# A hybrid layer (RWKV-7, S5, GLA, cross-attention, convolutional feed-forward) on one core: packed parameters, another order of the fillers, and two direct feed-forward pairs

## The chip, the core and the metric

One of the eight cores of a Trainium2 chip. PE is TensorE (matmul), DVE VectorE, ACT ScalarE, POOL GpSimd; SP issues most DMAs. The metric is the device time of one execution in microseconds.

## What is computed

One layer over x (1024 tokens x 1024) and mem (256 x 1024), all in float32:

```python
h = rms_norm(x, norm_mix)
p_rw, p_s5, p_gla, p_gate = split(h @ w_in)
y_rw  = rwkv7_mix(p_rw, ...)    # S = S*w + (S@-kk)(kk*a)^T + v k^T, per head of 64, along the tokens
y_s5  = s5_mix(p_s5, ...)       # 32 groups of 16 channels, 64 complex diagonal states each; gelu, glu
y_gla = gla_mix(p_gla, ...)     # chunked gated linear attention
gates = sigmoid(p_gate)         # three gates of 1024 columns
x = x + (sum_i gates_i * (y_i @ w_branch_i)) @ w_out
x = x + cross_attention(rms_norm(x, norm_xattn), rms_norm(mem, norm_mem), ...)
u = conv3(rms_norm(x, norm_ffn) @ w_up) + conv_b          # depthwise along the tokens
x = x + (silu(u[:, :2816]) * u[:, 2816:]) @ w_down
return rms_norm(x, norm_final)
```

## The kernel before

**Products.** Each float32 operand is split into a rounded part and a remainder (`hi`, `lo`), and a product is three: hi*hi, hi*lo, lo*hi (`mm3`, L163 to L165). A weight unit (`wunit`, L156) is a DMA into `wraw`, a cast on ACT into `whi` (L147), and a subtraction on DVE into `wlo` (L148). `fm_block` fills ps_fm, 128 columns x 1024 tokens, with 96/2 = 48 products of 128x512 from two units. PSUM holds two tiles of 128x1024 (`psd`: ps_fm, ps_q, ps_dn) and four of 128x512 (`psm`: most others). Small products of float32 operands as they are (S5's, RWKV's) go through PE in two passes.

**Stages.** (1) The opening, to about 75 us: keys and values of mem, norm and transposition of x into hT. (2) S5, to about 330: u blocks; then for each half of the groups the transposed input maps (hs, ps_ht), the driven states (ps_in), a scan on DVE (L538 to L541), for each of two quads the gains ga (seven DVE operations through `cmul`, L330 to L337 and L559), the short kernels (ps_k, kp, a round through DRAM into M), and the outputs ps_y. (3) GLA. (4) RWKV: `rw1`, the triangular solve `rw_solve` on DVE, and `rw2`: 16 groups of four chunks with the products vl, w1, x1, z (z = vl*w1 + w1, needs the evacuated vl and w1) and qm (needs the evacuated z, `qz`), then four steps on the state (ps_p, L1013 to L1016; L1019 and L1020 scale the state for the next), then a norm. (5) Output projection and attention. (6) Feed-forward up, as 22 pairs of blocks: pair 0 direct, pairs 1 to 21 in Winograd form (`wino_product`, 84 products a pair instead of 96). (7) The down projection.

**What sets the order.** The tile scheduler writes each engine's instructions into one fixed order from the program's order and priorities; each engine works them off in that order and waits for semaphores. So work that does not depend on a stage is written as a *filler* inside it: 24 gate blocks of 48 products (`gate_block`), 11 of them in S5 (`filler`), 3 in `rw1`, 10 after it beside the solve; in `rw2`, `fill()` puts in the branch products once for each group. L156's loads, the gates' stores and S5's small transfers share SP's queue.

**Small loads.** `vectors` loads 15 parameter vectors as rows, transposes them on PE (ps_v) and copies them to columns; `conv_consts` does the same for the convolution, `s5_states` for S5's parameters (ps_s, ps_c, ps_d). mem is loaded, and transposed by 16 PE transposes (ps_t).

Of the kernel before, what the change touches and what calls it, by code (L numbers as in the profile page):

```python
# [9 lines left out]
F32 = mybir.dt.float32  # L10
# [11 lines left out]
NB = NFF // 2  # L22
EPS = 1e-6
# [17 lines left out]
class Trunk:  # L41
# [44 lines left out]
    def vectors(self, p):  # L86


        nc, cp, A = self.nc, self.cp, self.A
        rows = [("nmem", A["norm_mem"], 8), ("nmix", A["norm_mix"], 8), ("mu", A["rw_mu"], 14), ("w0", A["rw_w0"], 4),  # L90
                ("a0", A["rw_a0"], 4), ("kk", A["rw_k_k"], 4), ("ka", A["rw_k_a"], 4), ("rk", A["rw_r_k"], 4),
                ("lnw", A["rw_ln_w"], 4), ("lnb", A["rw_ln_b"], 4), ("bglu", A["s5_b_glu"], 4),
                ("nxa", A["norm_xattn"], 8), ("nffn", A["norm_ffn"], 8), ("gkb", A["gla_gk_b"], 2), ("gnorm", A["gla_norm"], 1)]
        nrow = sum(n for _, _, n in rows)
        self.vc = cp.tile([128, nrow], F32, name="vc")
# [3 lines left out]
        self.vo = {}  # L99
        vr = [p.tile([n, 128], F32, name=f"vr{n}") for n in (16, nrow - 16)]  # L100

        def load(part, t, r0):
            for name, ap, n in part:
                o = self.vo[name] = sum(x[2] for x in rows[:[x[0] for x in rows].index(name)])
                flat = ap if len(ap.shape) == 1 else ap.rearrange("a b -> (a b)") if len(ap.shape) == 2 \
                    else ap.rearrange("a b c -> (a b c)")
                nc.sync.dma_start(t[o - r0:o - r0 + n, :], flat.rearrange("(n p) -> n p", p=128))

        def columns(t, r, n):
            ps = self.psm.tile([128, 512], F32, tag="m", name="ps_v")  # L110
# [150 lines left out]
    def start(self, pool):  # L261

        self.hT = self.new_T(pool, "hT")
        with ExitStack() as c2:
# [17 lines left out]
            mem = [load(self.A["mem"][0, tt * 128:tt * 128 + 128, :]) for tt in range(2)]  # L282
            other_vectors = self.vectors(p)

            self.mT = {(k, l): p.tile([128, 256], F32R, name=f"mT{k}{l}") for k in range(8) for l in range(2)}
            self.to_fm(mem, "nmem", lambda k, l: self.mT[k, l][:])
            self.mrs = scales(mem)
            ones = p.tile([128, 128], F32, name="ones")
            self.nc.gpsimd.memset(ones[:], 1.0)
            self.mrb = p.tile([128, 256], F32, name="mrb")  # L290
            dg = p.tile([128, 256], F32, name="dg")
            for i in range(2):
                self.nc.vector.tensor_scalar(dg[:, i * 128:i * 128 + 128], self.ident[:], self.mrs[:, i:i + 1], None, op0=ALU.mult)
            ps = self.psm.tile([128, 512], F32, tag="m", name="ps_rb")
            self.nc.tensor.matmul(ps[:, :256], ones[:], dg[:], start=True, stop=True)
            self.nc.scalar.copy(self.mrb[:], ps[:, :256])
# [8 lines left out]
            self.kv_k(0)  # L305
            self.kv_k(1)
            load_x()
# [3 lines left out]
            norm_half(0)  # L311
            self.kv_v(0)
            norm_half(1)
            for j in range(1, 4):
                self.kv_v(j)
# [41 lines left out]
    def s5(self, filler):  # L357
# [4 lines left out]
        with ExitStack() as c1:  # L362
            po = self.pool(c1, "s5o")
            YT = [po.tile([128, T], F32, name=f"s5yt{b}") for b in range(4)]
            with ExitStack() as c2:
                p = self.pool(c2, "s5p")
                self.s5_states(p, YT, KD, UD)
                filler()
# [15 lines left out]
    def s5_states(self, p, YT, KD, UD):  # L384
# [3 lines left out]
        rows = p.tile([48, 128], F32, tag="kp", name="s5rows")  # L388
        ls = p.tile([48, 2], F32, name="s5ls")
        nc.sync.dma_start(rows[0:16, :], A["s5_a_re"][0].rearrange("(g r) n -> g (r n)", r=2))  # L390
        nc.sync.dma_start(rows[16:32, :], A["s5_a_im"][0].rearrange("(g r) n -> g (r n)", r=2))
        nc.sync.dma_start(ls[32:48, :], A["s5_log_step"][0].rearrange("(g r) -> g r", r=2))
        v.tensor_copy(rows[32:48, :].rearrange("p (r n) -> p r n", r=2), ls[32:48, :].unsqueeze(2).to_broadcast([16, 2, 64]))
        ps = self.psm.tile([128, 512], F32, tag="m", name="ps_s5")
        nc.tensor.transpose(ps[:, :48], rows[:, :], ident[:48, :48])
        par = p.tile([128, 48], F32, name="s5par")
        v.tensor_copy(par[:], ps[:, :48])
        ar, ai, lst = par[:, 0:16], par[:, 16:32], par[:, 32:48]
        B = [p.tile([128, 16, 16], F32, name=f"s5b{i}") for i in range(2)]
        C = [p.tile([128, 16, 16], F32, name=f"s5c{i}") for i in range(2)]  # L400
        for i, (bn, cn) in enumerate((("s5_b_re", "s5_c_re"), ("s5_b_im", "s5_c_im"))):
# [4 lines left out]
            for t in range(4):  # L406
                nc.tensor.transpose(ps[0:64, t * 128:t * 128 + 128], cr[:, t, :], ident[:])
# [1259 lines left out]
```

## Time and profile before

| | |
|---|---|
| time, median of 3 runs | 2225.42 us (2224.3 to 2226.51) |
| profiled execution | 2228.63 us, span 2226.9 |
| busy | PE 95%, PE's weight loads 78%, DVE 65%, ACT 43%, POOL 9% of the span |
| mean granted TensorE clock | 0.988 of full speed |
| DMA | 286.65 MB, mean 129 GB/s |

The profile is of one execution. Busy time of an engine is an average over stages; a wait is put down to the instruction that ended it last. The granted clock is the share of TensorE's full 2.4 GHz that the chip gave it; its other level is 1.2 GHz (0.5).

### The profile page before, as it was taken

To read this page: it belongs to the slowest core of one execution; us is meant where nothing else is said; L and a number is where in the kernel's file an instruction comes from. 1 tells how busy PE (TensorE), PEld (TensorE's weight loads), DVE (VectorE), ACT (ScalarE), POOL (GpSimd) and SP (SyncE) were. 2 spreads that over 40 slices of the span, in tenths; PEclk is the share of its full clock that TensorE was granted. 3 is DMA by queue.
4 is the path that set the end of the run, shared out by engine and by line. 5 is a ranking of instruction groups with operands and counts; after the bars stand their busy time and mean duration, and the time that the engine had idled before them with its cause. 6 is when DMAs were issued, how large, how long until landed. Compare 5 with 4: busy or idle time off the path is not lost.

```text
span 2226.9 us, 29866 instructions
## 1 busy us (share of the span) xinstructions
PE 2123.9 (95%) x10704; PEld 1738.8 (78%) x10704; DVE 1447.8 (65%) x2870; ACT 961.0 (43%) x1667; POOL 196.3 (9%) x292
## 2 busy tenths in 40 slices
PE   7999989999999999999999999999899999988997
PEld 7878779888888888888788787877677777766886
DVE  7783733554667761667686656657777777777756
ACT  6324243553554431333343544446444444453452
POOL 1000000001211221002200000000011111110000
PEclk9999999999999999999999999999999999999999
DMA  7423331112334465665564232332565566588332
GB/s 246 137 88 95 94 97 54 29 52 67 134 112 128 135 186 152 171 157 141 136 214 148 87 104 72 89 119 81 137 157 159 139 150 128 123 241 286 104 96 102
DMA packets 318878, 286.65 MB, mean 129 GB/s; under 512 B 92532, under 2 KB 253129, under 8 KB 318729
## 3 DMA queue, kind: packets, MB, share of 16 engines
q1 hardware_dynamic: 291385, 207.64, 32.7%
q0 software_dynamic: 27344, 77.08, 12.7%
q8 instruction: 85, 1.39, 0.3%
q14 instruction: 64, 0.52, 0.1%
HBM read 190.32 MB, written 94.34 MB: 128 GB/s over the span
## 4 chain that ended last, share of the span: by engine, by line
PE 78%; DVE 10%; ACT 4%; DMA 4%; issue 2%; SPq 1%; DVEq 0%; ACTq 0%
PE ps_fm L163 10%; PE ps_fm L165 10%; PE ps_fm L164 10%; PE ps_q L1287 5%; PE ps_q L1288 5%; PE ps_q L1289 5%; PE ps_dm L1461 4%; PE ps_dn L1461 4%; PE ps_tm L163 3%; PE ps_tm L165 3%; PE ps_tm L164 3%; DVE wlo L148 2%; PE ps_g L868 1%; ACT whi L147 1%; DMA araw<-d_act 1%
## 5 line engine op out<-in xcount | busy, mean ns | idle before, releaser
L148 DVE TENSOR_TENSOR wlo<-wraw,whi 128x512 fp32r<-128x512 f32 (+1 forms) x318 | 219.7, 692 | 278.4 <-ACT whi L147 276.1
L147 ACT CAST whi<-wraw 128x512 fp32r<-128x512 f32 (+1 forms) x318 | 196.5, 619 | 472.0 <-PE ps_fm L164 283.0
L163 PE MATMUL ps_fm<-hT,whi 128*128 128x512 f32 x800 | 319.1, 399 | 0.0
L164 PE MATMUL ps_fm<-hT,whi 128*128 128x512 f32 x800 | 317.5, 397 | 0.0
L165 PE MATMUL ps_fm<-hT,wlo 128*128 128x512 f32 x800 | 317.4, 397 | 0.0
L163 PEld LDWEIGHTS ps_fm<-hT,whi 128*128 128x128 f32 x800 | 151.8, 190 | 33.1 <-issue 1.2
L165 PEld LDWEIGHTS ps_fm<-hT,wlo 128*128 128x128 f32 x800 | 151.5, 189 | 33.1 <-issue 0.6
L164 PEld LDWEIGHTS ps_fm<-hT,whi 128*128 128x128 f32 x800 | 151.8, 190 | 32.6 <-issue 0.8
L1287 PE MATMUL ps_q<-a,whi 128*128 128x512 f32 x336 | 134.9, 402 | 13.1 <-ACT u L1362 5.6
L1289 PE MATMUL ps_q<-a,wlo 128*128 128x512 f32 x336 | 134.1, 399 | 1.1 <-DVE wlo L148 1.1
L1288 PE MATMUL ps_q<-a,whi 128*128 128x512 f32 x336 | 134.0, 399 | 0.0
L1300 DVE SCALAR_TENSOR_TENSOR c<-u,cvn,c 128x1023 f32<-128x1023 f32 x84 | 107.7, 1283 | 22.2 <-ACT c L1298 20.8
L1309 POOL DMA_DIRECT2D d_act<-c x77 | 65.9, 862 | 438.5 <-DVE c L1304 320.5
L165 PE MATMUL ps_tm<-whi,a 128*128 128x512 f32 x256 | 101.3, 396 | 0.0
L1461 PE MATMUL ps_dn<-whi,b 128*128 128x512 f32 x312 | 98.6, 393 | 2.8 <-ACT whi L147 2.8
L147 ACT CAST whi<-s 128x512 fp32r<-128x512 f32 x84 | 52.1, 620 | 105.3 <-PE ps_q L1288 80.9
L147 ACT CAST b<-araw 128x512 fp32r<-128x512 f32 x72 | 44.7, 620 | 101.3 <-PE ps_dn L1461 37.6
L1287 PEld LDWEIGHTS ps_q<-a,whi 128*128 128x128 f32 x336 | 64.4, 192 | 29.5 <-ACT u L1362 6.9
L1461 PE MATMUL ps_dm<-whi,b 128*128 128x512 f32 x264 | 84.0, 398 | 2.4 <-ACT whi L147 2.4
L148 DVE TENSOR_TENSOR wlo<-s,whi 128x512 fp32r<-128x512 f32 x84 | 57.6, 688 | 36.3 <-ACT whi L147 35.3
L163 PE MATMUL ps_fm<-a,whi 128*128 128x512 f32 x192 | 78.7, 410 | 2.3 <-ACT whi L147 2.2
L148 DVE TENSOR_TENSOR b<-araw,b 128x512 fp32r<-128x512 f32 x72 | 49.6, 690 | 47.1 <-ACT b L147 46.9
(551 smaller groups left out, 5058.9 us busy)
## 6 DMA issues: line engine op xcount, KB each, us to landing
wraw<-in_w_in SPq DMA_DIRECT2D x104, 256.0 KB
araw<-d_act SPq DMA_DIRECT2D x77, 256.0 KB
d_act<-c POOLq DMA_DIRECT2D x22, 768.0 KB, 7.6
d_gate<-gate SPq DMA_DIRECT2D x24, 512.0 KB
gsg<-d_gate SPq DMA_DIRECT2D x24, 512.0 KB
wraw<-in_ffn_w_up SPq DMA_DIRECT2D x46, 256.0 KB
d_act<-c POOLq DMA_DIRECT2D x11, 1024.0 KB, 6.1
d_act<-c POOLq DMA_DIRECT2D x44, 256.0 KB, 5.1
```

Of the source, the lines that this page charges most:

```text
L147: self.nc.scalar.copy(hi, src)
L148: self.nc.vector.tensor_tensor(lo, src, hi.bitcast(F32), op=ALU.subtract)
L163: nc.tensor.matmul(ps, lh, rh, start=first, stop=False)
L164: nc.tensor.matmul(ps, lh, rl, start=False, stop=False)
L165: nc.tensor.matmul(ps, ll, rh, start=False, stop=last)
L868: nc.tensor.matmul(ps[:, j * 128:j * 128 + 128], BD[i][:, ci, :], AR[:, :, ci * 64:ci * 64 + 64], start=True, stop=True)
L1287: nc.tensor.matmul(ps, hi[:, s], t[0][:], start=first and k == 0, stop=False, skip_group_check=True)
L1288: nc.tensor.matmul(ps, hi[:, s], t[1][:], start=False, stop=False, skip_group_check=True)
L1289: nc.tensor.matmul(ps, lo[:, s], t[0][:], start=False, stop=last and k == 3, skip_group_check=True)
L1300: v.scalar_tensor_tensor(c[:, d:], src[:, :T - d], cw(2 - d), c[:, d:], op0=ALU.mult, op1=ALU.add)
L1309: to = lambda n0, n1, h, **kw: nc.gpsimd.dma_start(st(n0, n1), src[h].to_broadcast([128, n1 - n0, 512]), **kw)
L1461: nc.tensor.matmul(o, a[x][:, s], w[y], start=first and k == 0, stop=last and k == 2, skip_group_check=True)
```

## The change

1. *Packed parameters.* The host lays the 15 vectors out as one array of columns (128x81), the convolution's constants as another (128x176), S5's as a third (`s5_par`, 128x1076, 551 KB, the first load of all), and passes mem transposed (`memT`, 1 MB) beside mem. The transposes of these leave PE. Keys are copied out of PSUM at once, into eight tiles, and scaled and stored later.
2. *S5.* The gains and short kernels of both quads now come before the scan; 13 gate blocks (before: 11) stand at set places.
3. *RWKV.* `rw2_prods` is cut in three, with a filler behind x1 and one behind the norm; the step of the group before goes between z and qm.
4. *Feed-forward.* Two direct pairs, whose convolution reads PSUM itself; 20 Winograd pairs.
5. *Down projection.* The first bank of accumulators is in `psm`, the second in `psd`.

```diff
+ND = 2
...
     def vectors(self):
+        nc.sync.dma_start(self.vc[:], A["cols"])
...
+            raw = [p.tile([128, 2, 256], F32, name=f"memT{u}") for u in range(4)]
...
+                self.nc.scalar.mul(self.mT[k, 0][:], t, g)
+                self.nc.vector.scalar_tensor_tensor(self.mT[k, 1][:], t, g, self.mT[k, 0][:].bitcast(F32), op0=ALU.mult, op1=ALU.subtract)
...
-            o = self.st.tile([128, 256], F32, tag="ko", name="ko", bufs=2)
-            nc.vector.tensor_tensor(o[:], ps[:, :256], self.mrb[:], op=ALU.mult)
-            nc.gpsimd.dma_start(self.d_k[c:c + 128, :], o[:])
+            o = self.kvp.tile([128, 256], F32, tag="ko", name="ko", bufs=8)
+            (nc.vector.tensor_copy if q else nc.scalar.copy)(o[:], ps[:, :256])
+            self.keys.append(o)
...
     def s5_states(self, p, pk, YT, KD, UD, fill):
...
+            fill(2)
...
+            def kernels(qd):
...
+                return GA, M
+            GA, M0 = kernels(0)
+            G0 = gains(GA)
+            GA, M1 = kernels(1)
+            fill(3)
             X = S[:, :, :, 1:129]
...
+            fill(1)
             for qd in range(2):
...
+                G, M = (gains(GA), M1) if qd else (G0, M0)
...
                 for g2 in range(2):
-                    todo.append((pr, hf * 2 + g2, self.rw2_prods(p, g2 * 4, t, R, c3)))
-                    if len(todo) > 1:
+                    z, qm = self.rw2_prods(p, g2 * 4, t, R, c3)
+                    fill()
+                    z()
+                    if todo:
                         step()
+                    todo.append((pr, hf * 2 + g2, qm()))
+                    norm()
+                    fill()
...
+        for b in range(ND):
+            cs = []
+            for i in range(2):
+                blk = i * NFF + b
+                ps = self.fm_block(A["ffn_w_up"][0][:, blk * 128:blk * 128 + 128], rhs, 8, by_half=b == 0)
+                c = self.xt(6 - 2 * b + i, "c")
+                conv(b, i, ps, c, self.cv, ((0, 512), (512, T)) if b == 0 else ((0, T),))
+                cs.append(c)
+            finish(b, cs)
...
-            for b in range(1, NFF):
+            for b in range(ND, NFF):
...
-            upto = -(-len(early) * g // 13) if g <= 13 else len(early) + -(-len(late) * (g - 13) // 3)
+            upto = -(-len(early) * g // 26) if g <= 26 else len(early) + -(-len(late) * (g - 26) // 6)
...
-                    self.gate_block(*gates[11 + pr])
+                    self.gate_block(*gates[13 + pr])
...
-            for g in gates[14:]:
+            for g in gates[16:]:
```

In all PE has 18 instructions fewer (9717 for 9735, with 12 products more in the feed-forward block), DVE 13, ACT 7, and SP 19 DMAs fewer. The lines of the new kernel are some 20 to 34 lower.

How the order moves, at three places. DVE in S5's first half, at the end of the scan (sc, s5s), before; cm and ga are the gains, kp the kernels' evacuation:

```order
L538 TENSOR_TENSOR sc_1646<-s5s,s5l 128x16x63
L539 TENSOR_TENSOR sc_1647<-s5s,s5l 128x16x63
L540 TENSOR_TENSOR sc_1646<-sc_1646,sc_1647 128x16x63
L148 TENSOR_TENSOR wlo<-wraw,whi 128x512
L541 TENSOR_TENSOR s5s<-s5s,sc_1646 128x16x63
L331 TENSOR_TENSOR cm_1660<-s5pw_1190,s5c_1102 128x576
L330 TENSOR_TENSOR cm_1659<-s5pw_1189,s5c_1101 128x576
L332 TENSOR_TENSOR ga_1657<-cm_1659,cm_1660 128x576
L335 TENSOR_TENSOR cm_1664<-s5pw_1189,s5c_1102 128x576
L336 TENSOR_TENSOR cm_1665<-s5pw_1190,s5c_1101 128x576
L337 TENSOR_TENSOR ga_1658<-cm_1664,cm_1665 128x576
L559 TENSOR_SCALAR ga_1658<-ga_1658 128x576
```

and in the new order, ahead of the scan:

```order
L479 COPY s5s<-ps_in 128x2x2x128 x2
L312 TENSOR_TENSOR ga_1638<-cm_1640,cm_1641 128x576
L315 TENSOR_TENSOR cm_1645<-s5pw_1125,s5pk 128x576
L316 TENSOR_TENSOR cm_1646<-s5pw_1126,s5pk 128x576
L317 TENSOR_TENSOR ga_1639<-cm_1645,cm_1646 128x576
L486 TENSOR_SCALAR ga_1639<-ga_1639 128x576
L310 TENSOR_TENSOR cm_1681<-s5pw_1125,s5pk 128x576
L115 TENSOR_TENSOR wlo<-wraw,whi 128x512
L495 SCALAR_TENSOR_TENSOR kp<-e_1065,s5pk,ps_k 128x16
L496 COPY kp<-ps_k 128x112
L311 TENSOR_TENSOR cm_1682<-s5pw_1126,s5pk 128x576
L312 TENSOR_TENSOR ga_1679<-cm_1681,cm_1682 128x576
```

The gains and kp stood behind the scan; they now stand ahead of it, among the copies of the driven states.

PE in RWKV's second half, from one group's z to its first steps, before:

```order
L979 MATMUL ps_z<-qw_8188,qvl 128x128 x4
L163 MATMUL ps_fm<-a_7869,whi 128x512
L164 MATMUL ps_fm<-a_7870,whi 128x512
L165 MATMUL ps_fm<-a_7869,wlo 128x512
L163 MATMUL ps_fm<-a_7875,whi 128x512
L979 MATMUL ps_qm<-qz,wa_7939 128x128
L1013 MATMUL ps_p<-qx_8043,qz 128x128
L1014 MATMUL ps_p<-wv_7926,R_7969 128x128
L1016 MATMUL ps_p<-s_0_0_7952,qqm 128x128
L979 MATMUL ps_qm<-qz,wa_7939 128x128 x3
```

and in the new order, in a group of the first half (ps_fm is filler):

```order
L130 MATMUL ps_fm<-a_7848,whi 128x512
L131 MATMUL ps_fm<-a_7849,whi 128x512
L132 MATMUL ps_fm<-a_7848,wlo 128x512
L952 MATMUL ps_z<-qw_8615,qvl 128x128
L994 MATMUL ps_p<-qx_8490,qz 128x128
L995 MATMUL ps_p<-wv_7863,R_8451 128x128
L952 MATMUL ps_z<-qw_8615,qvl 128x128 x3
L994 MATMUL ps_p<-qx_8490,qz 128x128
L995 MATMUL ps_p<-wv_7863,R_8451 128x128
L997 MATMUL ps_p<-s_2_1_7899,qqm 128x128
```

The filler between z and qm is now ahead of z; between z and qm stand products of the step.

DVE in the feed-forward block, where pair 0's convolution (L1300, cv) and the u of the first Winograd pair (L1368) stand, before:

```order
L1300 SCALAR_TENSOR_TENSOR c_14352<-u_14063,cv,c_14352 128x1022
L148 TENSOR_TENSOR wlo<-s_14402,whi 128x512
L1300 SCALAR_TENSOR_TENSOR c_14356<-u_14127,cv,c_14356 128x1023
L1274 TENSOR_TENSOR s_14518<-b_0_1_14512,wraw 128x512
L1300 SCALAR_TENSOR_TENSOR c_14356<-u_14127,cv,c_14356 128x1022
L148 TENSOR_TENSOR wlo<-s_14406,whi 128x512
L1274 TENSOR_TENSOR s_14520<-s_14518,b_0_1_14510 128x512
L1274 TENSOR_TENSOR s_14522<-b_0_1_14510,b_0_1_14512 128x512
L1304 TENSOR_TENSOR c_14352<-c_14352,c_14356 128x1024
L1368 TENSOR_TENSOR u_14253<-ps_q,u_14399 128x512
L148 TENSOR_TENSOR wlo<-b_0_1_14510,whi 128x512
```

and in the new order, around the convolution of the last direct block (L1283, from PSUM):

```order
L1283 SCALAR_TENSOR_TENSOR c<-ps_fm,cv,c 128x1023
L115 TENSOR_TENSOR wlo<-s_14312,whi 128x512
L1283 SCALAR_TENSOR_TENSOR c<-ps_fm,cv,c 128x1022
L1255 TENSOR_TENSOR s_14459<-b_0_1_14361,wraw 128x512
L115 TENSOR_TENSOR wlo<-s_14314,whi 128x512
L1287 TENSOR_TENSOR c<-c 128x1024
L115 TENSOR_TENSOR a_14301<-t_14283,a_14300 128x512
L1334 TENSOR_TENSOR u_14322<-ps_14321,p_14340 128x512
```

The direct pairs' convolutions now precede the first Winograd sums' remainders; the u of the first Winograd pair (L1352) comes 11 rows behind these.

## Rows read from the trace of the kernel before

**Rows 1.** The page's first part: busy time of PE in us, its share of the span, and its instructions.

```profile
PE 2123.9 (95%) x10704; PEld 1738.8 (78%) x10704; DVE 1447.8 (65%) x2870; ACT 961.0 (43%) x1667; POOL 196.3 (9%) x292
```

**Rows 2.** PE's timeline: start and duration in us, engine, line, operation, out<-in. The first and the last start of 31 products of 128x512 that follow one another.

```profile
953.22 0.39 PE L165 MATMUL ps_fm<-a,wlo 128*128 128x512 f32 x1
...
960.16 0.39 PE L165 MATMUL ps_fm<-a,wlo 128*128 128x512 f32 x1
```

**Rows 3.** Busy time by stretches of the span (start:end, length; for each engine its busy us and its instructions; the mean granted clock of TensorE, DMA's busy share, GB/s).

```profile
0.00:75.00 75.00, 60.22 (x472) 58.02 (x473) 52.56 (x129) 48.75 (x89) 9.58 (x25) 1.00 0.74 229
75.00:330.00 255.00, 234.29 (x1208) 189.66 (x1207) 153.71 (x363) 84.41 (x119) 5.81 (x11) 0.96 0.33 96
880.00:1112.00 232.00, 219.65 (x1392) 186.31 (x1391) 159.38 (x395) 76.18 (x156) 27.10 (x28) 1.00 0.59 151
1537.00:1600.00 63.00, 51.98 (x201) 39.70 (x200) 50.76 (x76) 32.63 (x52) 3.99 (x5) 0.92 0.33 88
1950.00:2050.00 100.00, 88.57 (x358) 68.55 (x358) 71.75 (x102) 43.75 (x70) 10.05 (x12) 0.97 0.89 272
```

**Rows 4.** PE's waits by what ended them: us in total, how often, the longest.

```profile
PE ps_k L563 <- DVE ga L332: 9.9, 2, 5.1
...
PE ps_v L111 <- DMA vr<-in_norm_mix: 6.6, 1, 6.6
PE ps_qm L979 <- DVE qz L997: 6.1, 6, 2.3
...
PE ps_q L1287 <- DVE u L1368: 5.1, 1, 5.1
PE ps_t L254 <- DVE hn L1165: 4.6, 4, 3.9
...
PE ps_ht L513 <- DVE hs L332: 2.6, 1, 2.6
PE ps_fm L163 <- DVE ko L1114: 2.6, 3, 1.8
PE ps_y L586 <- DMA s5m<-s_k: 2.5, 1, 2.5
PE ps_q L1287 <- ACT whi L147: 2.5, 1, 2.5
...
PE ps_y L585 <- ACT s5g L577: 1.9, 1, 1.9
PE ps_fm L163 <- ACT s5h L147: 1.8, 1, 1.8
...
PE ps_z L979 <- DVE qw L990: 1.1, 3, 0.4
```

**Rows 5.** The same table as in rows 3, for two stretches of the opening and for the one in which DVE works out S5's parameters.

```profile
0.00:10.00 10.00, 1.73 (x7) 1.32 (x7) 3.63 (x19) 5.44 (x8) 1.73 (x11) 1.00 0.85 258
10.00:20.00 10.00, 9.18 (x60) 8.69 (x60) 6.91 (x22) 6.84 (x15) 0.00 (x0) 1.00 0.92 289
84.00:107.00 23.00, 23.00 (x100) 18.56 (x100) 20.38 (x119) 6.56 (x13) 1.09 (x2) 1.00 0.28 92
```

**Rows 6.** The timelines of DVE and of ACT around S5's scan in the first half: the scan's first operation, the first of ga after it (L331), and ACT's four copies of the scanned states.

```profile
129.52 1.23 DVE L538 TENSOR_TENSOR sc<-s5s,s5l 128x1024 f32<-128x1024 f32 x1
...
161.93 0.75 DVE L331 TENSOR_TENSOR cm<-s5pw,s5c 128x576 f32<-128x576 f32 x1
```

```profile
162.05 4.21 ACT L553 COPY s5s<-s5s 64x1024 f32<-64x1024 f32 x4 [5.91 <-DVE s5s L541]
```

**Rows 7.** The timeline of all engines in RWKV's second half: one link of the state (L1016 is the product with the state, L1019 and L1020 scale it), and a z with its qz and qm.

```profile
950.12 0.39 PE L1016 MATMUL ps_p<-s,qqm 128*128 128x128 f32 x2
...
950.61 0.29 DVE L1019 TENSOR_SCALAR s<-ps_p,rw_pc 64x64 f32<-64x64 f32 x1 [0.45 <-PE ps_p L1016]
...
950.93 0.31 ACT L1020 ACTIVATE s<-ps_p,rw_pc 64x64 f32<-64x64 f32 x1 [1.42 <-DVE s L1019]
...
951.84 0.39 PE L1016 MATMUL ps_p<-s,qqm 128*128 128x128 f32 x2
```

```profile
963.21 1.13 PE L979 MATMUL ps_z<-qw,qvl 128*128 128x128 f32 x8
...
964.38 0.69 DVE L997 TENSOR_TENSOR qz<-ps_z,qw 128x512 f32<-128x512 f32 x1 [1.31 <-PE ps_z L979]
...
965.13 0.49 PE L979 MATMUL ps_qm<-qz,wa 128*128 128x128 f32 x2
```

**Rows 8.** The timelines of POOL, of SP's queue and of PE ahead of RWKV's second half: the store of the solved triangles, the last load of the first group's ring, the first group's first product.

```profile
839.07 0.54 POOL L907 DMA_DIRECT2D rw_x<-sx  x1 [26.90 <-DVE sx L905]
```

```profile
860.22 0.63 SPq L962 DMA_DIRECT2D wv<-rw_tm  x1
```

```profile
884.33 1.05 PE L979 MATMUL ps_vl<-wx,wn 128*128 128x128 f32 x8
```

**Rows 9.** DVE's groups by line and shape (busy us, mean ns of one, idle time before) for RWKV's second half and for the feed-forward block; then the first Winograd product on PE, and DVE's operation that ended the longest wait in the block.

```profile
L1088 DVE TENSOR_TENSOR a<-gsg,ps_fm 128x512 f32<-128x512 f32 x16 | 10.3, 684 | 1.3 <-PE ps_fm L165 1.1
```

```profile
L148 DVE TENSOR_TENSOR wlo<-s,whi 128x512 fp32r<-128x512 f32 x84 | 57.6, 688 | 36.3 <-ACT whi L147 35.3 <-PE ps_q L1288 1.0
```

```profile
1546.43 0.42 PE L1287 MATMUL ps_q<-b,whi 128*128 128x512 f32 x1
```

```profile
1580.68 0.68 DVE L1368 TENSOR_TENSOR u<-ps_q,u 128x512 f32<-128x512 f32 x1
```

More of the change, by code (lines that the diff above doesn't have):

```diff
@@ L311, in start @@
             norm_half(0)
+            self.mrs = scales([load(self.A["mem"][0, tt * 128:tt * 128 + 128, :]) for tt in range(2)])
             self.kv_v(0)
             norm_half(1)
+            ones = p.tile([128, 128], F32, name="ones")
+            self.nc.gpsimd.memset(ones[:], 1.0)
+            mrb = p.tile([128, 256], F32, name="mrb")
+            dg = p.tile([128, 256], F32, name="dg")
+            for i in range(2):
+                self.nc.vector.tensor_scalar(dg[:, i * 128:i * 128 + 128], self.ident[:], self.mrs[:, i:i + 1], None, op0=ALU.mult)
+            ps = self.psm.tile([128, 512], F32, tag="m", name="ps_rb")
+            self.nc.tensor.matmul(ps[:, :256], ones[:], dg[:], start=True, stop=True)
+            self.nc.scalar.copy(mrb[:], ps[:, :256])
+            for j, o in enumerate(self.keys):
+                self.nc.vector.tensor_tensor(o[:], o[:], mrb[:], op=ALU.mult)
+                self.nc.gpsimd.dma_start(self.d_k[j * 128:j * 128 + 128, :], o[:])
             for j in range(1, 4):
@@ L355, in exp_exact, with s5 @@
         return q
-    def s5(self, filler):
+    def s5(self, c1, pk, fill):
         nc, A, v = self.nc, self.A, self.nc.vector
@@ L417, in s5_states @@
+        ar, ai, lst, dcol = (pk[:, o:o + n] for o, n in ((0, 16), (16, 16), (32, 16), (48, 4)))
+        B, C = ([pk[:, o + i * 256:o + i * 256 + 256].rearrange("p (g c) -> p g c", g=16) for i in range(2)] for o in (52, 564))
         e16 = p.tile([128, 16], F32, name="e16")
@@ L1496, in ffn_down @@
                 add(i, 0, bank["A"][i], ALU.add)
-            bank["B"] = [self.psm.tile([128, 512], F32, tag="m", name="ps_dm")[:] for _ in range(4)]
+            bank["B"] = second()
             product("s1", "n1", bank["B"], True, False, (load_w("b22"),))
@@ L1509, in ffn_down @@
                 add(4 + i, 1, bank["A"][i], ALU.subtract, True)
-            bank["B"] = [self.psm.tile([128, 512], F32, tag="m", name="ps_dm")[:] for _ in range(4)]
+            bank["B"] = second()
             product("a12", "b21", bank["B"], True, True)
@@ L1544, in run, with fill @@
         self.d_v = self.dr.tile([256, D], F32, name="d_v")
-        self.start(self.pool(left, "hT"))
-        self.s5(lambda: [self.gate_block(*g) for g in gates[:11]])
+        hT, c1 = self.pool(left, "hT"), ExitStack()
+        pk = self.pool(c1, "s5k").tile([128, 1076], F32, name="s5pk")
+        nc.sync.dma_start(pk[:], A["s5_par"])
+        self.start(hT)
+        todo = gates[:13]
+        def fill(n):
+            for _ in range(min(n, len(todo))):
+                self.gate_block(*todo.pop(0))
+        self.s5(c1, pk, fill)
         self.gla()
```

256 lines of the change are left out of this document (103 added, 153 removed).

## The prediction

> **What bounds the kernel now.** I read the profile from the engines down to single waits. The page's first part gives the bound: PE is busy for 2123.9 us, 95% of the span of 2226.9 [rows 1]. The profiled execution took 2228.63 us, its span and 1.7 us around it, 3.2 us over the median of 2225.42; a term worked out from its trace is subtracted from the median. Where every cover holds, PE starts a 128x512 product each (960.16 - 953.22) / 30 = 0.231 us [rows 2]; so only three things shorten this kernel: fewer products, less waiting on PE, and less time at the half clock. The table by stretches says where the last two lie [rows 3]. From 75 to 330 us, the S5 stage, PE idles 255 - 234.3 = 20.7 us at a mean granted clock of 0.96; 4% of 255 us is another 10.2 us. In RWKV's second half (880 to 1112) it idles 12.4 us, in the opening 75 us 14.8, in the first part of the feed-forward block (1537 to 1600) 11.0 us, and there the clock of 0.92 costs 5.0 more. Around 1950 to 2050 DMA is 0.89 busy. [...]
>
> **The change part by part.**
>
> *Opening, +3 us.* Removed: 16 transposes of mem and the one of the gains (some 17 x 0.13 = 2 us of PE), and the waits on them: PE's first instruction came at 6.6 us behind a row load, and 2.6 us were lost on ko, whose evacuation waited for the scale [rows 4]. Now ko is a plain copy into eight buffers. Added: memT is loaded as well as mem (1.05 MB more), and the S5 block of 551 KB, formerly loaded later in pieces, stands first on SP's queue. That is 1.6 MB where DMA ran at 258 to 289 GB/s [rows 5]: 6 us if nothing hides it. In the new SP order 4 x loads (2.1 MB) also stand ahead of the third key block's weights; 0.55 + 1.05 + 1.05 + 2.1 + 0.26 MB at 0.27 MB/us is 18 us, some 5 us after PE would be done with two blocks. The queue's later half has room (0.74 busy over 75 us, rows 3). PE's idle of 14.8 us should become about 14, and the work 2 to 3 us less; bounds -4 (all of the 6 us lost) and +7. The Trainium skill (DMA: Bandwidth & Descriptors, Specifications) limits one core to some 358 GB/s of HBM; no stretch here reaches that, and by it the 1.6 MB take an estimated 4.5 us, which would make this term +4.5.
>
> *S5, +20 us.* Before, DVE ran the scan from 129.52 to 161.93 us and only then the seven operations of ga, each 0.67 to 0.8 us start to start, for which ps_k waited 5.1 us; ACT's four copies of 4.21 us stood behind the scan, too [rows 6]. The 9.9 us at ps_k, 2.6 at ps_ht, 4.4 at ps_y and 1.8 at s5h make 18.7 of the 20.7 us [rows 4]. ps_ht now has 192 products (44 us) ahead of it; DVE's chain of parameters, which filled 20.4 us of it between 84 and 107 us [rows 5], takes some 30 us with the subtractions. At ps_k the new DVE order puts copies, two subtractions and three operations ahead of the first ga (some 5.6 us) against 11 products, 16 ps_in and 8 transposes (some 5.2 us): up to 0.5 us left, four times. ps_y stands 143 + 11 products behind the last kernel (35 us); scan with its subtractions and the copies are 32.4 + 4.2 = 36.6 us: 1 to 2 us left in each half, perhaps with one half clock (1.7 us). 40 products (9 us) now cover the s5h chain. Kept: 2 + 4 + 3 and 2 of small ones; 30.9 - 11 = 20. Bounds: 28 with nothing kept, 8 if each half keeps a 4 us stop and its clock at both ps_k and ps_y.
>
> *RWKV, +6 us, and -1 ahead of it.* qm starts 1.9 us after z's first product at the best (963.21 and 965.13, rows 7), since qz stands between them on DVE from 964.38 for 0.69 us; z itself takes 0.9 us of the 1.9. ps_qm's 6.1 us idle and its 2.3 us stop near 1108 with a half clock of 1.7 us are to be had, and 1.1 us of ps_z [rows 4]. But the new order puts the filler between x and z; behind z stand mostly one step of three products (0.67 us) and 0 to 3 fillers, so in half of the 16 groups some 0.4 us stays. 6.1 + 1.7 + 1.1 - 8 x 0.4 = 5.7. Bounds 0 and 11. Ahead of it two gate blocks fewer (96 products, 22 us) cover the triangular solve: before, its result left at 839.07, the last load of the first group's ring was issued at 860.22, PE arrived at 884.33 [rows 8]. It now arrives 22 us earlier, at 862: about 0 to 2 us of stop; taken 1, bounds 0 and 6.
>
> *Feed-forward, +11 us.* A second direct pair costs 96 products for 84, +12 x 0.231 = 2.8 us, less the about 1 us that each Winograd pair loses: +1.7. Gained: PE reached the first ps_q at 1546.43 and then stood 2.5 us for whi and 5.1 us for the u of L1368 [rows 4], which DVE ran at 1580.68, behind the convolution, sums and the 1024-wide product of pair 0 [rows 9]; these and small stops are the 11.0 us of the stretch [rows 3]. Gone are 10.4 of them and 4 of the 5.0 us of clock. With 96 products more ahead of it, PE gets there 22 us later, while DVE has 30 operations more at 0.6 and 1.2 us less 8 that move away: about 5 us in hand. The stop at hn (4.6 us in four, rows 4) keeps its order and stays. New: the convolution of the last direct block reads ps_fm until about 1577, and the second ps_q wants that bank at about 1577: 0 to 3 us, taken 1.5. 10.4 + 4 - 1.7 - 1.5 = 11; bounds 4 and 13. On that read: DVE's 128x512 operations take 684 ns with a PSUM source (L1088) and 688 ns without one (L148) [rows 9], so I charge nothing. The Trainium skill (VectorE: DVE Perf Modes, Rules for kernel authors) speaks against it: copy to SBUF first if there are many operations; by its table of fixed costs the 12 operations would take an estimated 0.065 us more each, and the sum would be 0.8 us less. The rows do not agree with that, and I follow them.
>
> *Down projection, 0.* The accumulators change places between two pools, but PE waited there for whi behind araw loads and order and loads are the same. Bounds -3 and +4. The constants' transposes near 1400 are two.
>
> Sum: 3 + 20 + 6 - 1 + 11 + 0 = 39 us; 2225.4 - 39 = **2186 us**.
>
> **The rivals.**
>
> *A, part of the stops form anew (-5 to -30, say 2206).* DVE takes its instructions in order; each cover above is within 1 to 2 us of what it covers, and a late first ga, a late scan and the bank at the second ps_q each bring the half clock back. For it: 32.6 us of filler against 36.6 us of scan. Against it: any single one costs 2 to 4 us. Three or four of them, and an opening bound by DMA, take 19 us: 2206.
>
> *B, slower.* The 60 links of RWKV's state go from ps_p over DVE's and ACT's s back to the next ps_p. At 950.12 and 951.84 a link takes 1.72 us on PE; its chain ends at 950.93 + 0.31 = 951.24 and, with a handover, needs some 1.25 us [rows 7]. The order now has seven links with only five small products between (1.34 us). If the spread fills put one 128x512 operation (0.69 us) ahead of s on either queue in every link, that is up to 60 x 0.69 = 41 us, and with a half clock here and there 45: it decides above 0.65 us a link, and the time is 2186 + 45 = 2231. Against it: s keeps its high priority, and most links keep 1.56 us and more.
>
> *C, nothing comes of it.* The filler is one stock: what S5 gets, the solve and the rest lose. It would take stops of 39 us elsewhere; the stretches that lend it (1112 to 1525, 540 to 880) hardly idle. Time 2225.
>
> *D, more than forecast.* All upper bounds but the opening's: 3 + 28 + 11 + 13 + 2 = 57 us, 2168.
>
> **How the numbers follow.** The forecast, -30 to -52 us, 0.58; A 0.23; D 0.08; C 0.05; B 0.06. The range takes the forecast and most of A: 2168 (D's figure) to 2212 (A with one more term lost). 0.2%, 4.5 us, is about what this measurement can tell from no change. Faster by more: 0.58 + 0.08 + 0.22 of A = 0.88; slower: B, 0.06; within it 0.06. The likeliest case decides the time, 2186.
>
> **What would show it.** In the trace of the changed kernel: ps_k's wait below 2 us in all and the S5 stretch's clock at 0.98 or more; ps_y's wait below 5 us; qm's idle halved while z's is gone; the first ps_vl without a stop over 2 us; no stop for the u of the first Winograd pair; the first product near 8 us and the last of the opening near 71. The prediction is wrong if ps_y or ps_k keeps a half clock in both halves, if ps_p waits for s in many links, or if the opening ends later than 75 us.

## The result and the profile after

The changed kernel takes **2209.87 us** (median of 4, 2208.78 to 2213.87) against 2225.97 (4 runs): a ratio of 0.9932, 95% interval 0.9918 to 0.9945. It is faster by 16 us where 39 were forecast. 2209.87 lies inside the range, near its upper end and near rival A's figure. The profiled execution took 2213.87 us, 4.0 over its median, so sizes of 4 us below are not read from this trace alone.

Boundaries on PE (the start of the last product of a kind) cut both profiled executions into the same stretches; all in us. One gate block is 11.05 (88.6 - 66.5 is two of them).

| stretch | before | after | gain |
|---|---|---|---|
| start to the last product with s5h | 330.0 | 327.1, with 2 more gate blocks | 2.9 + 22.1 |
| of it, the opening (last key and value product) | 74.0 | 73.2 | 0.7 |
| GLA and RWKV's first loop | 465.7 | 465.8 | -0.1 |
| gate blocks up to the first ps_vl | 88.6 | 66.5, 2 fewer | 0 |
| RWKV's second half and attention, to the last ps_pt | 558.9 | 571.5 | **-12.6** |
| to the last transpose of hn | 92.8 | 92.2 | 0.6 |
| feed-forward, to the last ps_q | 459.6 | 457.9 | 1.7 |
| down projection, to PE's last product | 220.7 | 220.0 | 0.7 |

So S5 gave 24.3 and RWKV's second half took half of it back. Of its 12.6 us some 5 belong to this one execution: two other executions with the same instructions in the same order there (e3 and e4 below) took 566.3 and 566.9. PE's line of the page's first part, against [rows 1]:

```profile
PE 2121.5 (96%) x10686; PEld 1741.7 (79%) x10686; DVE 1445.0 (65%) x2857; ACT 950.8 (43%) x1660; POOL 196.0 (9%) x292
```

The same stretches as in [rows 3], but for the feed-forward's, which begins 12 us earlier, as the block does now, and ends at the same time:

```profile
0.00:75.00 75.00, 60.62 (x458) 58.03 (x459) 53.03 (x132) 49.45 (x94) 9.33 (x25) 0.98 0.78 243
75.00:330.00 255.00, 250.51 (x1310) 202.63 (x1309) 157.12 (x362) 86.13 (x123) 5.94 (x12) 1.00 0.36 105
880.00:1112.00 232.00, 215.82 (x1315) 186.41 (x1314) 160.17 (x390) 72.97 (x150) 27.02 (x28) 0.97 0.61 153
1525.00:1600.00 75.00, 66.54 (x268) 51.86 (x267) 56.40 (x83) 34.17 (x53) 5.28 (x6) 0.95 0.45 116
1950.00:2050.00 100.00, 89.98 (x360) 70.54 (x359) 75.89 (x114) 41.25 (x68) 8.03 (x10) 0.93 0.91 284
```

S5 idles 4.5 us for 20.7 and runs at the full clock. RWKV's second half idles 16.2 for 12.4 and its clock fell to 0.97. PE's waits, against [rows 4]:

```profile
PE ps_fm L130 <- ACT whi L114: 13.4, 4, 8.8
...
PE ps_p L994 <- ACT s L1001: 5.5, 8, 1.4
PE ps_z L952 <- DVE rs_b L193: 4.6, 2, 3.0
PE ps_t L221 <- DVE hn L1146: 4.5, 4, 3.9
...
PE ps_q L1268 <- DVE u L1352: 2.9, 1, 2.9
...
PE ps_y L551 <- ACT s5s L541: 2.5, 2, 1.2
...
PE ps_fm L130 <- DVE c L1283: 2.3, 1, 2.3
PE ps_z L952 <- DVE rs_y L194: 2.2, 2, 2.0
PE ps_z L952 <- DVE rs_b L192: 2.0, 1, 2.0
PE ps_qm L952 <- DVE qz L974: 1.8, 1, 1.8
PE ps_y L551 <- ACT s5g L507: 1.8, 2, 0.9
```

Of the first line, 8.8 us stand before the first product of all and 2.47 in the opening. ps_k, ps_ht, ps_v and ko are gone from the list, ps_qm fell from 6.1 to 1.8. New are ps_p behind s, ps_z behind the norm's rs_ operations, and two stops in the feed-forward block.

**How z comes to wait.** The timeline of after shows the longest of these (start, duration, engine, line, operation; in brackets the idle time before and what ended it):

```profile
1094.54 1.22 DVE L1081 TENSOR_TENSOR gsg<-gsg,ps_fm 128x1024 f32<-128x1024 f32 x1
1095.80 1.29 DVE L1083 TENSOR_TENSOR gsg<-gsg,a 128x512 f32<-128x512 f32 x2
1096.52 1.22 ACT L114 CAST a<-gsg 128x512 fp32r<-128x512 f32 x2 [3.03 <-DVE gsg L1083]
1097.17 0.69 DVE L115 TENSOR_TENSOR a<-gsg,a 128x512 fp32r<-128x512 f32 x1
1097.65 0.58 ACT L959 COPY qvl<-ps_vl 128x512 f32<-128x512 f32 x1
...
1099.31 0.68 DVE L963 COPY qw<-ps_w 128x512 f32<-128x512 f32 x1
...
1100.13 0.76 PE L952 MATMUL ps_z<-qw,qvl 128*128 128x128 f32 x2 [3.00 <-DVE rs_b L193]
...
1101.83 0.77 PE L130 MATMUL ps_fm<-a,whi 128*128 128x512 f32 x1
```

The filler behind the last norm has left its evacuations (gsg, the cast and the subtraction of a) on both queues, ahead of qvl and qw, which z needs. ps_w's products began at 1095.18, its copy qw only at 1099.31: eight small rs_ operations of the norm and four wide ones stand between. The slot between x and z, which should hide this, is empty here: 17 pieces of filler were dealt over 26 slots. Behind the stop a 128x512 product takes 0.77 us instead of 0.39; the granted clock is 0.50 until about 1106.

z's three other long stops (1.60 us at 981.30, 1.95 at 996.78, 1.96 at 1034.18) have a second cause. The timeline of after shows it at the middle one:

```profile
993.33 2.49 POOL L1073 TENSOR_TENSOR a<-a,gsg 128x512 f32<-128x512 f32 x2 [4.84 <-DVE gsg L1072]
993.75 0.87 DVE L190 TENSOR_SCALAR rs_y<-rs_i 64x8 int32<-64x8 int32 x1
994.66 1.18 DVE L192 TENSOR_TENSOR rs_b<-rs_y 64x8 f32<-64x8 f32 x1
995.87 0.16 DVE L193 SCALAR_TENSOR_TENSOR rs_b<-rs_x,rs_b 64x8 f32<-64x8 f32 x1
995.96 0.68 DVE L963 COPY qw<-ps_w 128x512 f32<-128x512 f32 x1
...
996.78 0.60 PE L952 MATMUL ps_z<-qw,qvl 128*128 128x128 f32 x2 [1.95 <-DVE rs_y L194]
```

POOL works on the filler's a in two operations of some 1.25 us. Two small operations of the norm, ahead of qw in DVE's queue, start beside them and take 0.87 and 1.18 us, where 0.16 is usual (the last section). By these rows that is an estimated 0.87 + 1.18 - 2 x 0.16 = 1.7 of the 1.95 us. No run took this work off POOL, so what it is worth in the whole is not shown.

**How u comes to wait.** POOL's, DVE's and PE's timelines of after, in the feed-forward block:

```profile
1569.27 1.37 POOL L1292 DMA_DIRECT2D d_act<-c  x2 [20.18 <-DVE c L1287]
1576.09 1.29 POOL L1292 DMA_DIRECT2D d_act<-c  x1 [5.45 <-DMA d_act<-c]
```

```profile
1584.69 0.69 DVE L1334 TENSOR_TENSOR u<-ps,p 128x512 f32<-128x512 f32 x1 [5.88 <-DMA d_act<-c]
...
1586.64 0.51 PE L1268 MATMUL ps_q<-a,whi 128*128 128x512 f32 x1 [2.91 <-DVE u L1352]
```

Direct pair 1 leaves its result in tiles 4 and 5, and the second Winograd pair's u is to be written to 4. That tile is free only when pair 1's store has left it: two transfers, then an accumulating one that waits for both and is issued 6.8 us later. DVE idles 5.88 us for it, the u of the first Winograd pair stands behind, and PE stops 2.91 us with a half clock after it. The other stop, near 1535, is a bank of PSUM: DVE's convolution of a direct block still reads ps_fm, and PE waits 2.3 us for it.

### The profile page after: what moved, and what is told of

Same layout as the page of the kernel before. It is cut to its first block, busy times and chain, and to the rows that moved or that the text cites. A ratio compares the mean times of both kernels' runs of the same rounds, so it can differ in the third digit from the quotient of the medians.

```text
span 2211.9 us, 29747 instructions
## 1 busy us (share of the span) xinstructions
PE 2121.5 (96%) x10686; PEld 1741.7 (79%) x10686; DVE 1445.0 (65%) x2857; ACT 950.8 (43%) x1660; POOL 196.0 (9%) x292
## 4 chain that ended last, share of the span: by engine, by line
PE 48%; DVE 5%; DMA 3%; ACT 2%; issue 1%; SPq 0%; DVEq 0%; ACTq 0%; POOLq 0%
PE ps_q L1268 5%; PE ps_q L1269 5%; PE ps_q L1270 4%; PE ps_dm L1439 4%; PE ps_dn L1439 4%; PE ps_fm L130 3%; PE ps_fm L131 3%; PE ps_fm L132 3%; PE ps_tm L130 2%; PE ps_tm L132 2%; PE ps_tm L131 2%; DMA araw<-d_act 1%; PE ps L1268 1%; ACT whi L114 1%; DMA wraw<-in_w_branch 1%
## 5 line engine op out<-in xcount | busy, mean ns | idle before, releaser
L115 DVE TENSOR_TENSOR wlo<-wraw,whi 128x512 fp32r<-128x512 f32 x320 | 220.6, 692 | 269.8 <-ACT whi L114 265.0
L114 ACT CAST whi<-wraw 128x512 fp32r<-128x512 f32 x320 | 197.2, 620 | 458.0 <-PE ps_fm L131 282.1
L1268 PE MATMUL ps_q<-a,whi 128*128 128x512 f32 x320 | 128.0, 400 | 7.6 <-ACT u L1346 4.2
L1269 PE MATMUL ps_q<-a,whi 128*128 128x512 f32 x320 | 127.2, 397 | 0.0
L1270 PE MATMUL ps_q<-a,wlo 128*128 128x512 f32 x320 | 126.7, 397 | 0.0
L1283 DVE SCALAR_TENSOR_TENSOR c<-u,cvn,c 128x1023 f32<-128x1023 f32 x80 | 102.5, 1283 | 19.4 <-ACT c L1280 18.2
L130 PE MATMUL ps_fm<-b,whi 128*128 128x512 f32 x192 | 77.9, 406 | 2.4 <-DVE c L1283 2.3
```

The lines of the kernel that those rows point to most:

```text
L114: self.nc.scalar.copy(hi, src)
L115: self.nc.vector.tensor_tensor(lo, src, hi.bitcast(F32), op=ALU.subtract)
L130: nc.tensor.matmul(ps, lh, rh, start=first, stop=False)
L1268: nc.tensor.matmul(ps, hi[:, s], t[0][:], start=first and k == 0, stop=False, skip_group_check=True)
L1269: nc.tensor.matmul(ps, hi[:, s], t[1][:], start=False, stop=False, skip_group_check=True)
L1270: nc.tensor.matmul(ps, lo[:, s], t[0][:], start=False, stop=last and k == 3, skip_group_check=True)
```

## The experiments

Three questions: what takes RWKV's second half down, what the feed-forward change is worth, and what the opening's stop costs. The stage below is the stretch from the first ps_vl to the last ps_pt. Shares "13/3/8" are gate blocks in S5, in RWKV's first loop, and behind it. In brackets behind a time stand its ratio to the kernel before, timed on the same chip, and the ratio's 95% interval; not all rounds ran on one chip, so runs are compared by these ratios.

**e1: the old dependent products in the changed kernel.**

```diff
-                    z, qm = self.rw2_prods(p, g2 * 4, t, R, c3)
-                    fill()
-                    z()
...
-            upto = -(-len(early) * g // 26) if g <= 26 else ...
+            upto = -(-len(early) * g // 13) if g <= 13 else ...
```

> The changed kernel with RWKV's second half as before (products undivided, one filler a group). Theory Q (queues): the split itself costs the 12.6 us that the stage is longer in the changed kernel, since the filler behind the norm sets branch evacuations and norm operations ahead of qw and qvl on DVE and ACT; time 2197 us (-12 to -14), ps_z's loss back at about 5 us. Rival P (place): the stage is longer because it starts 25 us earlier and finds its loads and the solve late; the split is worth its forecast +6, and undoing it gives 2209 to 2216.

Measured 2211.92 (2206.85 to 2214.23; 0.9946, 0.9931 to 0.9961), stage 566.0. Undoing the split gives nothing back. But it was no clean undoing: the same source as before's was laid out in another order on DVE and ACT, and there qm waits 9.9 us and z 7.5. PE's waits of e1 in the stage:

```profile
PE ps_qm L945 <- DVE qz L963: 9.9, 6, 3.4
PE ps_z L945 <- DVE qw L956: 5.7, 5, 3.5
PE ps_z L945 <- DVE rs_y L190: 1.8, 1, 1.8
```

So the share of the gates, outside the stage, changes it.

**e2: one filler for each group, between x and z; e3: pair 1's results in tiles 2 and 3; e4: the old feed-forward block.**

```diff
# e2
                     norm()
-                    fill()
...
-            upto = -(-len(early) * g // 26) if g <= 26 else ...
+            upto = -(-len(early) * g // 13) if g <= 13 else ...
# e3
-                c = self.xt(6 - 2 * b + i, "c")
+                c = self.xt(6 - 4 * b + i, "c")
```

> The changed kernel with one filler a group, between x and z in every group, and none behind the norm. Theory Q: every z has its cover and nothing of a branch stands ahead of qw any more; ps_z's loss of 14.3 us falls to 3 or less, the whole to 2200 (-8 to -12). Rival S (state chain): ps_z's loss goes to ps_p, because the steps now stand without filler and wait for s on ACT; ps_p's loss rises from 15 to over 20 us and the time stays at 2207 to 2212.

> The changed kernel with the second direct pair's results in tiles x2 and x3 instead of x4 and x5, which the second Winograd pair's u takes. Theory T (tile): DVE's 5.9 us wait for the store of that pair goes, with it PE's 2.9 us at ps_q (u L1352) and the half clock behind it: 2205.5 (-4 to -5). Rival D (DVE load): DVE is that late by its own work; the wait moves by 1 us at most, 2209 to 2211.

> The changed kernel with the feed-forward block as before (one direct pair through SBUF, 21 Winograd pairs). By the traces the block's change is worth 1.6 us net: 2211.5 (+1 to +3). If the forecast's term of 11 us is there and is only hidden by something later, 2220.

e2: 2202.64 (0.9904, 0.9888 to 0.992), stage 564.6; with the slot before z always filled, the time that PE loses ahead of z's products beside a dense run falls from 14.3 to 6.5 us, not to the 3 of theory Q, and p's does not rise as rival S has it (17 and 16). e3: 2203.95 (0.991, 0.9894 to 0.9926): the stop for u is gone, the same 75 us hold more work. The stretch of e3 that answers to 1525:1600 of after:

```profile
1520.00:1595.00 75.00, 69.56 (x289) 54.69 (x288) 59.99 (x90) 36.84 (x58) 5.28 (x6) 0.98 0.45 116
```

e4: 2210.54 (0.9938, 0.9924 to 0.9953), no different from the changed kernel: as built, the new block is worth nothing that these runs can tell; with the free tile, by the ratios of e3 and e4, some 6 us.

**e5 and e6: the changed kernel with 11/3/10, with the old products and with the split ones; e7: the kernel before with the split alone; e8: e2 and e3 together.**

```diff
-        todo = gates[:13]
+        todo = gates[:11]
...
-            for g in gates[16:]:
+            for g in gates[14:]:
```

> The changed kernel with RWKV's second half as before and with the gate blocks shared out as before (11 in S5, 3 in rw1, 10 behind it). In this form PE, DVE and ACT have in that stage instruction for instruction the order of the kernel before, which the first undoing (13, 3, 8) did not have: there the scheduler laid the same source out otherwise. Theory O (order): the stage then takes what it took before, 559 us from the first ps_vl to attention's last ps_pt, against 566 to 571 in the changed kernel and its first undoing; time 2202 (-6 to -10 against the changed kernel). Rival P (the stage suffers from what runs ahead of it, loads and DRAM traffic): 2208 to 2212.

> The changed kernel with the gate blocks shared out as before (11, 3, 10), and the split RWKV stage, which the scheduler then lays out in another order than in the changed kernel. Theory O: the split is not worth one fixed amount; in this order ps_qm and ps_z lose less by my count of the places (2.8 against 3.8 us); 2200 to 2208. Rival Q (the split as such costs 7 us or more, through the fillers behind the norm): 2208 to 2212, like the changed kernel.

> The kernel before with the split RWKV stage alone (two fillers a group); its order in that stage is the same as in the run with 11, 3 and 10 gate blocks. The forecast gave the split +6: 2219. Theory Q: it costs 7: 2231. Theory O: as far from the kernel before as the run with the split and 11 gates stands from the one with the undivided stage and 11 gates, within 3 us.

> The changed kernel with one filler a group, between x and z, and with the second direct pair's results in tiles x2 and x3: both edits together. They lie in different stages and should add up: -7 (filler) and -6 (tile) give 2197. If one of them only moves a wait that the other one's stage gives back, 2201 to 2203.

e5: 2212.97 (0.9953, 0.9935 to 0.997), e6: 2219.26 (0.9976, 0.9966 to 0.9986), e7: 2227.3 (1.0016, 1.0005 to 1.0027), e8: 2201.64 (0.99, 0.9883 to 0.9918). e5's order in RWKV's second half is row for row before's, and its stage is 556.6: what e1 lost is back. But both e5 and e6 missed the whole times expected of them (2202, and 2200 to 2208), because S5 then lacks the two blocks; PE's waits of e5 in 75:330 show what they had covered:

```profile
PE ps_y L551 <- ACT s5s L541: 12.2, 2, 11.0
```

The split's stage is 560.1 in e6 and 561.3 in e7: 3.5 and 2.4 more than the old products under the same share. By the whole times the split costs 5 us there (e6 against e5) and 3.5 in e7. e8's ratio is 0.0032 under the changed kernel's; its two edits alone gave 0.0028 and 0.0022. They fall short of adding up, though with intervals of 0.0014 to 0.0018 to either side this is not told apart from a full sum.

**e9: 13 gate blocks in S5, yet 10 behind the first loop, with the old products and e3's tiles; e10: the same with e2's split; e11: the same with the changed kernel's split.**

```diff
-                if pr < 3:
-                    self.gate_block(*gates[13 + pr])
+                if pr == 2:
+                    self.gate_block(*gates[13])
...
-            for g in gates[16:]:
+            for g in gates[14:]:
```

> The changed kernel with the old dependent products, pair 1's results in the other tiles, and the 24 gate blocks as 13 in S5, 1 in the first RWKV loop, 10 behind it. On VectorE and ScalarE the order of the RWKV stage is then row for row that of the kernel before. Theory 'order': the stage's length follows from that order, 556 to 558.5 us where the changed kernel has 571.5, while S5's whole gain stays (328 to 330); the first loop is shorter by two gate blocks, 269 to 271 for 292.0, the run of gates behind it 88.6; total 2190 to 2198. Rival 'one stock': the two blocks were needed where they lay, the first loop gives up less than their 22.1 us (273 to 280), and the total is 2200 to 2206, no better than with the tiles alone (2204).

> As the last, but with the three products of a group taken apart and one filler block between x and z (none behind the norm). Theory 'order': another order on VectorE and ScalarE, so another length; the stage 557 to 565 by the runs with this split so far (560.1, 561.3, 564.1), total 2194 to 2202, that is no better than the old dependent products under the same share of gates. Rival 'the split pays once the evacuations are out of the way': the stage under 555, total under 2192.

> The changed kernel with its split products and both fillers of a group as they are, pair 1's results in the other tiles and the gate blocks shared 13 / 1 / 10. The RWKV stage's order is then that of the run with 11 gates in S5 and of the run with the split alone (560.1 and 561.3 us), another one than that of the changed kernel (571.5). Theory 'order': the stage 559.5 to 562, the total 2195 to 2200, so the share of the gates alone is worth 4 to 9 us against the run with the tiles alone (2203.95), and the split alone costs 2 to 5 against the old products under this share (2193.95). Rival 'the split costs what the changed kernel's stage lost': the stage 565 or more, total above 2202.

e9: **2193.95** (0.9854, 0.9839 to 0.9868), e10: 2196.52 (0.9862, 0.9846 to 0.9879), e11: 2198.96 (0.9878, 0.9862 to 0.9895). In e9 the first loop took 274.0, 3 to 5 us above what the theory said and within the rival's bounds, but the gate blocks behind it 1.6 less (87.0): 19.6 of the two blocks' 22.1 us came off there, 2.5 did not. The total is the theory's. PE's waits of e9 in its stage (860 to 1120):

```profile
PE ps_qm L945 <- DVE qz L963: 7.2, 7, 2.3
...
PE ps_p L979 <- ACT s L986: 0.8, 1, 0.8
PE ps_z L945 <- DVE qw L956: 0.7, 2, 0.4
```

and its S5 stretch, which kept the gain:

```profile
75.00:330.00 255.00, 251.41 (x1303) 203.55 (x1302) 156.40 (x362) 86.42 (x125) 6.81 (x13) 0.99 0.36 106
```

The same waits of e11 (859 to 1143) show the split's trade, qm for p and z:

```profile
PE ps_p L994 <- ACT s L1001: 4.2, 6, 1.8
...
PE ps_qm L952 <- DVE qz L974: 2.0, 2, 1.8
...
PE ps_z L952 <- DVE rs_b L193: 1.6, 1, 1.6
PE ps_z L952 <- DVE qw L963: 1.6, 2, 0.8
```

The stage of all of them, by the order in which its rows stand on PE, DVE and ACT (kernels of one letter have the same rows in the same order through RWKV's second half; in attention the rows of before and e7, which still transpose the convolution's constants there, stand partly otherwise):

| order | products | shares | stage in us |
|---|---|---|---|
| a | old | 11/3/10 (before, e5), 13/1/10 (e9, e12) | 558.9, 556.6, 557.8, 556.1 |
| b | split | 11/3/10 (e7, e6), 13/1/10 (e11) | 561.3, 560.1, 561.0 |
| c | split | 13/3/8 (after, e3, e4) | 571.5, 566.3, 566.9 |
| d | old | 13/3/8 (e1) | 566.0 |
| z only | split | 13/3/8 (e2, e8); 13/1/10 (e10) | 564.6, 564.1; 558.6 |

Under one order the stage varies by 3 us (c: 5); between orders of the same products by 5 to 11. The number of blocks behind the first loop goes with the order, whether S5 has 11 or 13 and the loop 1 or 3. So no run here changes the order and keeps that number. That the order is what costs the time is read from PE's stops: in the stage of after and of e1 each is ended by an operation of DVE or ACT, and none by a DMA. ACT's own waits for the branch weights do grow, from 3.9 us in before to 14.5 in after (first 300 us of the stage); whether these delay a copy that PE needs was not tested.

**e12: e9 with the weights of the third and fourth key blocks ahead of the x loads.**

```diff
             self.kv_k(0, us)
-            load_x()
             self.kv_k(1)
+            load_x()
```

> The run with old products, other tiles and 13 / 1 / 10, with the first four x loads behind the weights of the third and fourth key blocks instead of ahead of them; RWKV's order stays. Theory 'a place in the queue': the stop of 2.6 us near 20 us and the half clock behind it go, the opening ends 1.5 to 4 us earlier (last product near 70), total 2190 to 2192.5. Rival 'bytes': DMA is over 0.9 busy through the first 40 us, so the x loads come as much later as the weights come sooner, the stop moves to the norm's transposes, and the total stays 2193 to 2196.

2192.13 (0.9852, 0.9837 to 0.9868), the fastest, though not told apart from e9 by its interval. The trace bears out the place in the queue: the last product of the opening starts at 71.6 instead of 74.1 in e9. The stop near 20 us is gone; one of 1.82 us stands at 25.8 instead, and the granted clock stays at 1.00. PE's timeline in after shows the stop, and the answering 20 us of both:

```profile
20.08 0.39 PE L130 MATMUL ps_fm<-mT,whi 128*128 128x256 f32 x1 [2.47 <-ACT whi L114]
```

```profile
20.00:40.00 20.00, 19.51 (x150) 19.30 (x151) 12.73 (x30) 9.82 (x20) 0.00 (x0) 0.91 0.90 296
```

```profile
20.00:40.00 20.00, 17.67 (x146) 17.03 (x144) 11.49 (x29) 10.46 (x20) 0.00 (x0) 1.00 0.96 310
```

The first two are after's, the third is e12's: at the full clock PE needs less busy time for nearly the same products.

## Why the prediction was wrong

The terms of RWKV, the feed-forward block and the opening came out 18.6, 9.3 and 2.3 us short in the two profiled executions, S5's 4.3 us over.

- **S5, +20: right.** 24.3 measured. ps_k and ps_ht left the list, the clock is 1.00, and ps_y's waits of 2.5 and 1.8 are the "1 to 2 us left in each half". e5 and e6 confirm the cover from the other side: with 11 blocks in the new order PE stops 11.0 us at ps_y.
- **The solve, -1: 0.** PE came 25 us earlier (first ps_vl at 859.4 for 884.3), without a stop. Rival C's rule, that the filler is one stock, does not hold for the first loop: of the two blocks taken from there in e9, 19.6 of 22.1 us were gained. Taken from behind it, as in the changed kernel, they did cost the next stage time, as rival C says (next point).
- **RWKV, +6: this is the step that failed.** It was worked out as 6.1 + 1.7 + 1.1 less 8 x 0.4 for what stays at qm. The qm part held: 4.3 of the 6.1 us went. The rest of the term looked at PE's order alone: how many products stand behind z. What the filler leaves on DVE and ACT ahead of qvl, qw and s was not counted, and z and p lost more than qm gained: summed over the stage, the distance from the product ahead of them, beyond that in a dense run, was 5.1 and 9 us before, 14.3 and 17 after; qm's was 9.2 and is 3.5. What POOL holds up on DVE was not counted either. Rival B had the mechanism at s, priced at 60 links of 0.69 us; the trace has it at 8 links, 5.5 us in all, and it had 0.06. The runs split the -12.6 in two. The split itself costs 2.4 to 3.5 us of the stage at an equal share (b over a). The other 5 to 11 come with the 13/3/8 share, which the prediction took to be a matter of S5 and the solve alone: it has the scheduler lay the whole stage out anew (c over b, d over a). That the order changes, and that the stage's length goes with it, is shown; that it is the order, and not the number of blocks ahead of the stage by another way, is argued from PE's stops; by which rule the scheduler turns two gate blocks into that order is open.
- **Feed-forward, +11: 1.7. The second step that failed.** Its first half held: the wait for whi of 2.5 us [rows 4] is down to 0.5, and PE no longer waits for the u of the first Winograd pair behind pair 0's convolution (5.1 us). But it waits 2.9 us for that u behind another operation. "About 5 us in hand" counted DVE's operations and not the tile: a store must leave tile 4 before the next pair's u, which stands ahead in the queue, can be written to it. e3, which changes only the tile, brings some 5 us by the ratios. The other omission is the bank: 1.5 us was charged at ps_q (1.2 measured), none at ps_fm (2.3). Behind the stops of 2.9 and 2.3 us the granted clock is 0.5 for some 3 us each; 0.95 over 75 us is 3.7 us, so most of the 4 us of clock, counted as gained, was not.
- **Reading PSUM, nothing charged: right.** DVE's groups of after: the convolution's operation takes 1280 ns from PSUM (ps_fm) and 1284 from a tile (u).

```profile
L1283 DVE SCALAR_TENSOR_TENSOR c<-u,cvn,c 128x1023 f32<-128x1023 f32 x40 | 51.4, 1284 | 18.2 <-ACT c L1280 18.2
...
L1283 DVE SCALAR_TENSOR_TENSOR c<-ps_fm,cv,c 128x1023 f32<-128x1023 f32 x2 | 2.6, 1280 | 1.4 <-ACT c L1280 1.4
```

  The Trainium skill (VectorE: DVE Perf Modes, Rules for kernel authors) lets the kernel either accept the 1x rate with a PSUM source or copy to SBUF first if there are many operations; these rows do not bear out a price for reading PSUM here.
- **Opening, +3: 0.7.** The stop was foreseen (x loads ahead of the third key block's weights) and is 2.47 us; PE idles 14.4 us, where 14 were forecast. What failed is "the work 2 to 3 us less": PE is busy for 60.62 us instead of 60.22, since the clock of 0.98 behind that stop takes 1.5 us, for which the term had nothing. With the weights first, in e12, the opening's last product starts 2.4 us earlier than before.
- **The half clocks.** The bounds and rivals let each long stop bring a half clock. The traces show no such fixed link: in before a stop of 2.24 us at 994.4 left the granted clock at 1.00, and in after one of 1.44 us at 873.9 was followed by 0.50.
- **Rival A** (2206) came nearest by number, and by luck: two of its three stops, a late first ga and a late scan, did not form; only the bank did, with 1.2 us. (Rival D's 57 us hold 2 us that none of the bounds gives.)

Against the forecast of 39, e12 gains 33: in its trace S5's term (24.3) and most of the opening's (2.4) stand, and half of the feed-forward's (5.5); the RWKV term does not exist in any order that was tried.

## What to carry to other kernels

Where a scheduler lays out every engine's queue, a change in one stage can lay out another anew: read the order of the stages that were *not* meant to change before pricing them at zero, and if they moved, try a share of the filler that leaves them as they were. A filler between dependent products is paid for on the evacuating engines: count what it puts ahead of the operand copies there, not only PE's products. And before a stop is booked as gone, follow the buffer as well as the engine: who has read the tile last, and is that a store with a transfer behind a transfer?

## What was not expected of the hardware

Small operations of DVE wait for POOL. An operation of 64x8 that takes 0.16 us elsewhere in the stage took 1.19 in e1. DVE and POOL in e1's timeline:

```profile
981.77 2.49 POOL L1058 TENSOR_TENSOR a<-a,gsg 128x512 f32<-128x512 f32 x2 [1.26 <-issue]
982.86 0.20 DVE L188 TENSOR_SCALAR rs_x<-ym 64x8 f32<-64x8 f32 x1
983.10 1.19 DVE L189 TENSOR_SCALAR rs_i<-rs_x 64x8 int32<-64x8 int32 x1
```

POOL's row is two operations, one behind the other: the first ends at 983.04, the second at 981.77 + 2.49 = 984.26. L188 starts beside the first and ends at 982.86 + 0.20 = 983.06; L189 starts beside the second and ends at 983.10 + 1.19 = 984.29. Each ends within 0.03 us of the POOL operation beside which it started. It is no matter of integers: in after the float32 operation L192 took 1.18 us in the same way (the rows at 994.66 above).

Over the 14 traces this divides cleanly. Counted were DVE operations that start beside a POOL operation of 128x512 and by their usual duration would end before it. All 104 that have their sources in SBUF, reductions apart, were held to POOL's end; none of 67 with a source in PSUM (qw, qz, s and others) and none of 28 reductions was. In all, DVE lost 6.0 us by it in before, 8.5 in after, 8.3 in e1 and 0.8 in e10.

The Trainium skill (SBUF — State Buffer, SBUF: two separate sides) tells of a pair of ports that DVE and GpSimd hold one at a time, for a whole instruction; the trace agrees with that for L188 and L189. Work given to POOL is thus not free for a chain of small DVE operations beside it.
